# Norm 1 of a hybrid encoder step: five of nine token tiles transposed by DMA instead of by TensorE

## The chip, the cores and the metric

The kernel runs on one core of one Trainium2 chip. A core has five engines with queues of their own: TensorE (PE in the profile, its weight loads PEld), VectorE (DVE), ScalarE (ACT), GpSimd (POOL) and SyncE (SP), which here only issues DMAs. Each works through its own queue in order and waits for the others by semaphores. The DMAs that SP issues run on 16 DMA engines. The metric is the device time of one execution in microseconds (us), the median of several runs.

## The reference

One step of a hybrid streaming encoder layer for 1024 prompt tokens and 64 sample tokens, 1024 features, in float32. Cut to what bears on the change:

```python
def rms_norm(x, g):
    xf = x.astype(F32)
    y = xf * lax.rsqrt(jnp.mean(xf * xf, axis=-1, keepdims=True) + EPS)
    return y.astype(x.dtype) * g

def token_mixers(u, past, p, l):
    proj = u @ p['w_in'][l]                      # 7436 columns
    fox, dif, sb, gdn, gates = jnp.split(proj, SPLITS, axis=-1)
    ...                                          # three attentions and a gated delta rule over them
    merged = sum(gate[:, :, i] * (o @ wb[i]) for i, o in enumerate(branches))
    return merged @ p['w_out'][l], new_state

def trunk(x, caches, p):
        mix, st = token_mixers(rms_norm(x, p['norm1_g'][l]), past, p, l)
        x = x + mix
        x = x + swiglu(rms_norm(x, p['norm2_g'][l]), p['w_ffn_gate'][l], p['w_ffn_up'][l], p['w_ffn_down'][l])
    y = rms_norm(x, p['final_norm_g'])
```

## The kernel before

The tokens form nine tiles: eight of 128 prompt tokens (t = 0 to 7) and one of 64 sample tokens (t = 8). Every float32 operand of a large product is split into two float16 halves, a high part and the remainder, and a product is three matmuls (high by high, high by low, low by high). The products want the normalised input u with features on the partitions, so the kernel keeps it transposed in one buffer, `u1` (line 222), with its halves `uh` and `ul`, 8 blocks of 128 features by 1088 tokens.

Norm 1 is `rms_to` (line 188), called once a tile from the loop at line 237. ACT squares the row and sums it, POOL makes the reciprocal root, DVE multiplies (`u32`, natural layout, tokens on partitions). TensorE then transposes eight 128x128 blocks of `u32` in float32 into two PSUM banks (`ptu`, line 200). From each bank ACT copies the high half into `uh`, and DVE takes the remainder into `ul`. 

Right behind it stands the first user of u, the loop over tiles that makes 268 columns (`gemm_b`, lines 158 to 168; three matmuls for each of eight blocks, 24 a tile, into one of two PSUM buffers `pd`). Its results leave PSUM by two small DVE copies (`abf`, lines 275 and 276) and one ACT copy (`zt`); ACT takes a tanh of that (`zh`), DVE multiplies it twice, and SP writes it to DRAM (`zd`, line 286). `zt` and `zh` share four buffers, so a write that is late holds back a later ACT copy, and that a PSUM buffer. Then follows `gdn_project`, which reads all of u for 768 columns (matmuls of lines 183 to 185).

Beside this run: the loads of x and of weights by SP (lines 230 and 149), the split of weights into halves (`wh` by ACT, `wl` by DVE), and small constants: `gnb`, `lq`, `gsub`, loaded by SP and touched by DVE. The weights land in three buffers `w32`, so a load waits until DVE has split what its buffer held.

The program is written as one stream. A scheduler with a time model of its own then fixes the order in which each engine meets its instructions; that order is part of the built program, and nothing is reordered at run time between the instructions of DVE, ACT, POOL or SP. In the attention phases that follow, projections fill TensorE beside the attention, and DMA transposes like those of the change are in use already (`pt<-st`, `qt<-qd`, `gt<-stg`, and `X<-nsh`, `X<-nsl` in norm 2).

Of the kernel before, what the change touches and what calls it, by code (L numbers as in the profile page):

```python
# [9 lines left out]
F16 = mybir.dt.float16  # L10
# [3 lines left out]
ALU = mybir.AluOpType  # L14
# [3 lines left out]
P = 128  # L18
D = 1024
# [29 lines left out]
def rows(t):  # L49
    return P if t < 8 else SMP  # L50
# [3 lines left out]
def tile_hybrid_encoder(ctx, tc, i, o):  # L54

    nc = tc.nc
    act, vec, gps, pe, sync = nc.scalar, nc.vector, nc.gpsimd, nc.tensor, nc.sync


    def acopy(out, in_, scale=1.0):  # L60
        return act.activation(out, in_, AF.Copy, scale=scale)  # L61

    def stt(out, in0, s, in1, op0, op1):
        return vec.scalar_tensor_tensor(out=out, in0=in0, scalar=s, in1=in1, op0=op0, op1=op1)  # L64

    def tt(out, in0, in1, op, eng=None):
        return (eng or vec).tensor_tensor(out=out, in0=in0, in1=in1, op=op)

    def ts(out, in0, s1, s2, op0, op1=None, eng=None):
        if op1 is None:  # L70
            return (eng or vec).tensor_scalar(out=out, in0=in0, scalar1=s1, scalar2=None, op0=op0)  # L71
        return (eng or vec).tensor_scalar(out=out, in0=in0, scalar1=s1, scalar2=s2, op0=op0, op1=op1)
# [16 lines left out]
    def psc(name="psc"):  # L89
        return pp.tile([P, 512], F32, tag="s", name=name, bufs=3)  # L90
# [50 lines left out]
    def load_unit_(parts, n, kk, wh, wl, w32t=None):  # L141
        wh, wl = (a.rearrange("p (k c) -> p k c", k=8) for a in (wh, wl))
        for k0 in range(0, kk, 4):
            kn = min(4, kk - k0)
            w32 = w32t() if w32t else wp.tile([P, 4, BW], F32, tag="w32", name="w32", bufs=3)
            c = 0
            for src, r0, c0, w in parts:
                with tc.issue_after(ahead[0]) if ahead else ExitStack():
                    sync.dma_start(
                        w32[:, :kn, c:c + w],  # L150
                        src[r0 + k0 * P:r0 + (k0 + kn) * P, c0:c0 + w].rearrange("(k p) c -> p k c", p=P),
                    )
                c += w
            acopy(wh[:, k0:k0 + kn, :n], w32[:, :kn, :n], WS)
            stt(wl[:, k0:k0 + kn, :n], w32[:, :kn, :n], WS, wh[:, k0:k0 + kn, :n], ALU.mult, ALU.subtract)
        return wh, wl
# [28 lines left out]
            mm = pe.matmul(ps[:, :n], lhsT=b, rhs=xh[:, k, off:off + n], start=False, stop=(k == K - 1))  # L185
        return mm

    def rms_to(pool, xt, n, g_bc, outh, outl, tok):

        u32 = pool.tile([P, D], F32, tag="nu", name="u32", bufs=2)  # L190
        ss = pool.tile([P, 1], F32, tag="nss", name="ss", bufs=3)
        act.activation(u32[:n], xt[:n], AF.Square, accum_out=ss[:n])
        rs = pool.tile([P, 1], F32, tag="nrs", name="rs", bufs=3)
        ts(rs[:n], ss[:n], 1.0 / D, EPS, ALU.mult, ALU.add, eng=gps)
        tt(rs[:n], rs[:n], mh[:n], ALU.pow, eng=gps)
        stt(u32[:n], xt[:n], rs[:n], g_bc[:n], ALU.mult, ALU.mult)
        for q in range(2):
            ps = psc("ptu")
            for k in range(4):
                pe.transpose(ps[:, k * P:k * P + n], u32[:n, (4 * q + k) * P:(4 * q + k + 1) * P], ident[:n, :n])  # L200
            pv = ps.rearrange("p (k t) -> p k t", k=4)[:, :, :n]
            hi, lo = (a[:, 4 * q:4 * q + 4, tok:tok + n] for a in (outh, outl))
            acopy(hi, pv)
            tt(lo, pv, hi, ALU.subtract)
# [4 lines left out]
    def xrows(t):  # L209
        return xp[t * P:(t + 1) * P] if t < 8 else xs  # L210
# [12 lines left out]
    uh, ul = u1[:, 0], u1[:, 1]  # L223
    with tc.tile_pool(name="n1", bufs=1, reuse_waits="tile") as n1:
        g1 = n1.tile([P, D], F32, name="g1")
        xts = []
        with tc.high_priority():
            for t in range(NT):
                xt = n1.tile([P, D], F32, tag="xt", name="xt", bufs=6)
                early = sync.dma_start(xt[:rows(t)], xrows(t))  # L230
                xts.append(xt)
                if t == 0:
                    sync.dma_start(g1, i["norm1_g"][0].partition_broadcast(P))
                    wua = load_unit_([(w_in, 0, OFF_ABZ, 264), (w_in, 0, OFF_FOX + 768, 4)], 268, 8,
                                     *(wa.tile([P, 8 * 268], F16, name="wa" + q) for q in "hl"),
                                     lambda: wa.tile([P, 4, 268], F32, tag="wa32", name="wa32", bufs=2))
        for t in range(NT):
            rms_to(n1, xts[t], rows(t), g1, uh, ul, t * P)


    zd = tc.dram_tile([T, BW], F32, name="zd")
# [27 lines left out]
    for t in range(NT):  # L269
        n = rows(t)  # L270
# [45 lines left out]
    for t0, cols in (((0, 1, 2, 3), 0), ((4, 5, 6, 7), 512), ((9, 10, 8), 1024)):  # L316
        ps = psc("pct")
        c = 0
        for t in t0:
            n = SMP if t == 8 else P  # L320
# [792 lines left out]
    for bi, b in enumerate(order):  # L1113
# [18 lines left out]
        for d, (off, n) in [(d, PIECES[p]) for p in (0, 2, 1) for d in range(KD)] if last else \  # L1132
                [(d, p) for d in range(KD) for p in PIECES]:
            th = (brp if bi == 0 else gt_pool).tile([P, 364], F32, tag=("th0" if bi == 0 else "th"), name="thg",
                                                    bufs=(4 if bi == 0 else 12))
# [120 lines left out]
    with tc.tile_pool(name="ps2", bufs=1, space=PSUM) as pf:  # L1256
# [189 lines left out]
        for t in (8, 0, 1, 2, 3, 4, 5, 6, 7):  # L1446
            n = rows(t)
            ss = fp.tile([P, 2], F32, tag="fss", name="fss", bufs=4)
            xh = [x2[t][:n, c * HK:(c + 1) * HK] for c in range(2)]
            dst = o["y_prompt"][0, t * P:(t + 1) * P] if t < 8 else o["y_sample"][0]  # L1450
# [51 lines left out]
```

## Time and profile before

| what | value |
|---|---|
| time, median of 3 runs | 1857.35 us (1855.86 to 1864.47) |
| the profiled execution's own time | 1860.61 us |
| its span | 1858.8 us |
| TensorE busy | 1736.6 us, 93% |
| VectorE busy | 1251.2 us, 67% |
| ScalarE busy | 862.3 us, 46% |
| mean granted TensorE clock | 0.981 of full |

The span is from the first to the last instruction on the core; the execution's own time is 1.8 us longer. Busy shares are means over stages with different limits, so a change in one stage is read from that stage. In a timeline a row gives the start, the duration, the engine, the line, the operation with the tile it writes and the tiles it reads, and, in brackets, how long the engine stood idle before and what ended that. Names are the program's, with numbers left out: `u` stands for u32 and u1 both, which the shapes tell apart.

### The profile page before, as it was taken

The page shows a single profiled execution, that of the slowest core. Times are in us where ns is not written, and L with a number is a line of the kernel's source. Part 1 is how long each engine was busy: PE and PEld are TensorE (multiplying, and loading weights), DVE is VectorE, ACT ScalarE, POOL GpSimd, SP SyncE. Part 2 cuts the span into 40 slices and gives each one's busy share as a digit, 9 for nine tenths or more (in the row PEclk, how much of TensorE's full clock was granted, in tenths as well). Part 3 has the DMA queues.
Part 4 walks back from the last instruction along what each step waited for, and adds up shares of the span by engine and source line. Part 5 has one row for each costly group of instructions (what it writes and reads, how often), then busy time and mean ns, then how long its engine had stood idle before and what let it go on. Part 6 is the DMA issues. An engine that isn't in the chain of part 4 may idle for free.

```text
span 1858.8 us, 36758 instructions
## 1 busy us (share of the span) xinstructions
PE 1736.6 (93%) x14364; PEld 1229.3 (66%) x14364; DVE 1251.2 (67%) x2634; ACT 862.3 (46%) x1819; POOL 291.9 (16%) x443
## 2 busy tenths in 40 slices
PE   7979987788988889999998989999999999999998
PEld 5658875565655556666665578777758668577573
DVE  7547984997877667877746887757637456465465
ACT  6325564977865545655654633523304223133132
POOL 2102240001212212232222731000000000000002
PEclk9989999999999999999999999999999999999999
DMA  7247798889899976655857845512211113012112
GB/s 225 49 71 182 221 252 186 191 188 215 181 203 198 192 153 138 148 141 134 209 178 235 228 141 104 109 52 69 69 35 58 46 46 92 26 44 69 35 46 102
DMA packets 415941, 244.55 MB, mean 132 GB/s; under 512 B 270066, under 2 KB 393422, under 8 KB 415700
## 3 DMA queue, kind: packets, MB, share of 16 engines
q1 hardware_dynamic: 403304, 206.22, 46.2%
q0 software_dynamic: 12464, 35.99, 6.7%
q8 instruction: 112, 1.84, 0.4%
q14 instruction: 61, 0.50, 0.1%
HBM read 123.39 MB, written 60.81 MB: 99 GB/s over the span
## 4 chain that ended last, share of the span: by engine, by line
PE 63%; DMA 13%; DVE 11%; issue 4%; ACT 4%; SPq 2%; POOL 1%; DVEq 0%; POOLq 0%; ACTq 0%
PE po L1424 12%; DMA pt<-st 5%; PE pgs L184 4%; PE pgs L183 4%; PE pgs L185 4%; PE pb L1308 3%; PE pb L1307 3%; PE pb L1309 3%; PE pc L1308 2%; PE pc L1309 2%; PE pa L1309 2%; PE pc L1307 2%; PE pa L1307 2%; PE pa L1308 2%; DMA gt<-stg 2%
## 5 line engine op out<-in xcount | busy, mean ns | idle before, releaser
L183 PE MATMUL pgs<-u,wh 128*128 128x364 f16 (+1 forms) x768 | 245.3, 319 | 0.5 <-ACT ths L61 0.5
L185 PE MATMUL pgs<-u,wl 128*128 128x364 f16 (+1 forms) x768 | 245.2, 319 | 0.0
L184 PE MATMUL pgs<-u,wh 128*128 128x364 f16 (+1 forms) x768 | 245.0, 319 | 0.0
L1424 PE MATMUL po<-wh,hT 128*128 128x512 f16 (+1 forms) x792 | 238.2, 380 | 0.6 <-DVE x2a L64 0.5
L1424 PEld LDWEIGHTS <-hT 128*128 128x128 f16 (+1 forms) x1188 | 109.1, 99 | 120.1 <-issue 7.6
L64 DVE SCALAR_TENSOR_TENSOR x2a<-po,x2a 128x512 f32<-128x512 f32 x108 | 74.4, 689 | 141.1 <-PE po L1424 140.9
L61 ACT ACTIVATE wh<-w32f 128x1024 f16<-128x1024 f32 (+1 forms) x90 | 80.3, 926 | 160.6 <-PE po L1424 111.7
L1307 PE MATMUL pb<-X,wh 128*128 128x288 f16 (+1 forms) x528 | 147.1, 279 | 2.4 <-DMA X<-nsh 2.0
L64 DVE SCALAR_TENSOR_TENSOR wl<-w32f,wh 128x1024 f16<-128x1024 f32 (+1 forms) x90 | 94.6, 1065 | 79.8 <-ACT wh L61 79.8
L1308 PE MATMUL pb<-X,wh 128*128 128x288 f16 (+1 forms) x528 | 147.2, 279 | 0.5 <-DMA X<-nsl 0.5
L1309 PE MATMUL pb<-X,wl 128*128 128x256 f16 (+1 forms) x528 | 146.4, 279 | 0.0
L1424 PE MATMUL po<-wl,hT 128*128 128x512 f16 (+1 forms) x396 | 142.1, 379 | 0.0
L165 PE MATMUL pd<-wh,u 128*128 128x256 f16 (+1 forms) x456 | 128.3, 281 | 14.4 <-DVE ks L64 6.6
L1307 PEld LDWEIGHTS <-wh 128*128 128x128 f16 x1232 | 120.4, 98 | 31.0 <-issue 2.2
L1308 PEld LDWEIGHTS <-wh 128*128 128x128 f16 x1232 | 120.4, 98 | 30.1 <-issue 2.4
L1309 PEld LDWEIGHTS <-wl 128*128 128x128 f16 x1232 | 120.4, 98 | 27.5 <-issue 1.0
L184 PEld LDWEIGHTS <-wh 128*128 128x128 f16 x912 | 89.8, 98 | 60.3 <-issue 11.4
L166 PE MATMUL pd<-wl,u 128*128 128x256 f16 (+1 forms) x456 | 128.0, 281 | 0.0
L167 PE MATMUL pd<-wh,u 128*128 128x256 f16 (+1 forms) x456 | 128.0, 281 | 0.0
L183 PEld LDWEIGHTS <-wh 128*128 128x128 f16 x912 | 89.8, 98 | 50.6 <-issue 1.3
L185 PEld LDWEIGHTS <-wl 128*128 128x128 f16 x912 | 89.8, 98 | 49.8 <-issue 1.2
L71 POOL TENSOR_SCALAR fss<-fss 128x1 f32<-128x1 f32 (+1 forms) x9 | 2.0, 220 | 660.2 <-ACT fsq L1453 660.2
(396 smaller groups left out, 4625.1 us busy)
## 6 DMA issues: line engine op xcount, KB each, us to landing
w<-in_w_in_dram SPq DMA_DIRECT2D x56, 512.0 KB, 4.7
w32f<-in_w_ffn_gate_dram SPq DMA_DIRECT2D x20, 512.0 KB, 5.0
w32f<-in_w_ffn_up_dram SPq DMA_DIRECT2D x20, 512.0 KB, 3.9
w32f<-in_w_ffn_down_dram SPq DMA_DIRECT2D x20, 512.0 KB, 4.8
xt<-in_x_prompt_dram SPq DMA_DIRECT2D x8, 512.0 KB, 6.9
wb<-in_w_branch_dram SPq DMA_DIRECT2D x8, 512.0 KB, 4.6
w<-in_w_out_dram SPq DMA_DIRECT2D x8, 512.0 KB, 3.8
x2a<-in_x_prompt_dram SPq DMA_DIRECT2D x8, 512.0 KB, 6.1
```

Of the source, the lines that this page charges most:

```text
L61: return act.activation(out, in_, AF.Copy, scale=scale)
L64: return vec.scalar_tensor_tensor(out=out, in0=in0, scalar=s, in1=in1, op0=op0, op1=op1)
L165: pe.matmul(ps[:n, :N], lhsT=a, rhs=wh[:, k, :N], start=(k == 0), stop=False)
L166: pe.matmul(ps[:n, :N], lhsT=a, rhs=wl[:, k, :N], start=False, stop=False)
L167: pe.matmul(ps[:n, :N], lhsT=b, rhs=wh[:, k, :N], start=False, stop=(k == K - 1))
L183: pe.matmul(ps[:, :n], lhsT=a, rhs=xh[:, k, off:off + n], start=(k == 0), stop=False)
L184: pe.matmul(ps[:, :n], lhsT=a, rhs=xl[:, k, off:off + n], start=False, stop=False)
L185: mm = pe.matmul(ps[:, :n], lhsT=b, rhs=xh[:, k, off:off + n], start=False, stop=(k == K - 1))
L1307: pe.matmul(ps[:, :n], lhsT=wh[:, k], rhs=xh_, start=(start and k == 0), stop=False, skip_group_check=not start)
L1308: pe.matmul(ps[:, :n], lhsT=wh[:, k], rhs=xl_, start=False, stop=False, skip_group_check=not start)
L1309: mm = pe.matmul(ps[:, :n], lhsT=wl[:, k], rhs=xh_, start=False, stop=(k == 3), skip_group_check=not start)
L1424: pe.matmul(ps[h * n:h * n + n], lhsT=hts[k + h][:, a, tk:tk + n], rhs=w[:, k + h], start=(k == 0 and a == 0 and w is wh), stop=(k + nh >= ...
```

## The change

From tile 4 on, the split comes first and the transpose after it: ACT copies the whole `u32` tile to float16 in natural layout, DVE takes the remainder, and two DMA transposes, issued by SP, put the two halves into `uh` and `ul`. The staging tiles `ust` rotate over six buffers. Tiles 0 to 3 keep the old way.

```diff
-    def rms_to(pool, xt, n, g_bc, outh, outl, tok):
+    def rms_to(pool, xt, n, g_bc, outh, outl, tok, by_dma):
...
         stt(u32[:n], xt[:n], rs[:n], g_bc[:n], ALU.mult, ALU.mult)
+        if by_dma:
+            st = [pool.tile([P, D], F16, tag="nst", name="ust", bufs=6) for _ in range(2)]
+            acopy(st[0][:n], u32[:n])
+            tt(st[1][:n], u32[:n], st[0][:n], ALU.subtract)
+            for dst, src in zip((outh, outl), st):
+                sync.dma_start_transpose(out=dst[:, :, tok:tok + n], in_=src[:n])
+            return
         for q in range(2):
             ps = psc("ptu")
...
         for t in range(NT):
-            rms_to(n1, xts[t], rows(t), g1, uh, ul, t * P)
+            rms_to(n1, xts[t], rows(t), g1, uh, ul, t * P, t >= 4)
```

The scheduler places the new instructions among the old. On SP, behind the load of the constant `gsub`, there stood before the loads of weights (`w32`) and the writes of the first gate tiles (`zd`):

```order
L595 DMA gsub_726<-in_diff_subln_g_dram 128x64
L149 DMA w32_921<-in_w_in_dram 128x4x256
L149 DMA w32_1085<-in_w_in_dram 128x4x256
L286 DMA zd_331<-zt_387 128x256
L286 DMA zd_331<-zt_421 128x256
L149 DMA w32_1089<-in_w_in_dram 128x4x256
L149 DMA w32_1314<-in_w_in_dram 128x4x256
```

In the changed program SP has there, from the second pair of weight loads on (`ust_230` and `ust_231` are the high and low halves of tile 4, `243` and `244` of tile 5, `256` and `257` of tile 6, `269` and `270` of tile 7):

```order
L149 DMA w32_1045<-in_w_in_dram 128x4x256
L149 DMA w32_1049<-in_w_in_dram 128x4x256
L293 DMA zd_291<-zt_347 128x256
L293 DMA zd_291<-zt_381 128x256
L202 DMA_TRANSPOSE u1_103<-ust_244 128x8x128
L202 DMA_TRANSPOSE u1_103<-ust_256 128x8x128
L149 DMA w32_1274<-in_w_in_dram 128x4x256
L293 DMA zd_291<-zt_415 128x256
L202 DMA_TRANSPOSE u1_103<-ust_269 128x8x128
L202 DMA_TRANSPOSE u1_103<-ust_257 128x8x128
L202 DMA_TRANSPOSE u1_103<-ust_270 128x8x128
```

Ten transposes now stand among the loads and the gate writes; the high half of tile 7 is issued ahead of the low half of tile 6. Three more, of tile 4 and of tile 5's high half, stand right before the first of these rows, and the two of tile 8 behind the last.

On DVE, from the constant `lq` on, before (the numbers of `ptu` are the PSUM banks of tiles 5, 6 and 7, `u32_265` and `u32_286` the multiplications of tiles 6 and 7):

```order
L67 TENSOR_TENSOR lq_715<-lq_715 128x64
L67 TENSOR_TENSOR u1_103<-ptu_230,u1_103 128x4x128
L71 TENSOR_SCALAR gsub_726<-gsub_726 128x64
L67 TENSOR_TENSOR u1_103<-ptu_237,u1_103 128x4x128
L275 TENSOR_SCALAR abf_350<-pd_462 128x8
L276 TENSOR_SCALAR abf_350<-pd_462 128x4
L67 TENSOR_TENSOR zt_387<-zt_387,gnb_357 128x256
L67 TENSOR_TENSOR zt_421<-zt_421,gnb_357 128x256
L589 TENSOR_REDUCE lam_721<-lq_715 128x2
L64 SCALAR_TENSOR_TENSOR u32_265<-xt_133,rs_268,g1_107 128x1024
```

The same place on DVE in the changed program, where `wl` is the split of a weight tile and `u32_249` the multiplication of tile 6:

```order
L67 TENSOR_TENSOR lq_675<-lq_675 128x64
L71 TENSOR_SCALAR gsub_686<-gsub_686 128x64
L64 SCALAR_TENSOR_TENSOR wl_708<-w32_713,wh_707 128x1024
L282 TENSOR_SCALAR abf_310<-pd_422 128x8
L283 TENSOR_SCALAR abf_310<-pd_422 128x4
L64 SCALAR_TENSOR_TENSOR wl_876<-w32_877,wh_875 128x1024
L67 TENSOR_TENSOR zt_347<-zt_347,gnb_317 128x256
L67 TENSOR_TENSOR zt_381<-zt_381,gnb_317 128x256
L596 TENSOR_REDUCE lam_681<-lq_675 128x2
L67 TENSOR_TENSOR ust_244<-u32_236,ust_243 128x1024
L64 SCALAR_TENSOR_TENSOR zt_415<-zh_417,zt_415 128x256
L64 SCALAR_TENSOR_TENSOR u32_249<-xt_133,rs_252,g1_107 128x1024
```

Two weight splits now stand between `lq` and the low half of tile 5, and that half stands ahead of the multiplication of tile 6. On PE the 36 float32 transposes of the five tiles are gone, and the matmuls keep their order but for four of tile 7 that move up to where tile 6 begins. Behind this stage SP's order is the same for more than fifty DMAs and PE's for more than 2,000 rows; after that all engines meet the projections and the attention in a somewhat different order.

## Rows read from the trace of the kernel before

**Rows 1.** The page: span, and busy time of each engine.
```profile
span 1858.8 us, 36758 instructions
PE 1736.6 (93%) x14364; PEld 1229.3 (66%) x14364; DVE 1251.2 (67%) x2634; ACT 862.3 (46%) x1819; POOL 291.9 (16%) x443
```

**Rows 2.** Busy time by stage: start:end length, engines, PEclk, DMA share, GB/s.
```profile
core 0: us, PE busy (x) PEld busy (x) DVE busy (x) ACT busy (x) POOL busy (x), PEclk, DMA share, GB/s
0.00:50.20 50.20, 38.44 (x288) 30.83 (x288) 37.06 (x78) 30.92 (x61) 9.73 (x26) 0.97 0.68 216
50.20:113.00 62.80, 62.80 (x419) 40.74 (x419) 29.82 (x62) 18.22 (x39) 9.65 (x15) 1.00 0.45 63
...
290.00:490.00 200.00, 162.58 (x1562) 119.28 (x1561) 160.05 (x282) 150.62 (x290) 18.18 (x29) 0.94 0.87 194
490.00:640.00 150.00, 134.98 (x1495) 87.84 (x1493) 106.31 (x334) 92.25 (x220) 33.12 (x53) 0.97 0.96 196
```

**Rows 3.** The same view: two stretches of norm 1, one of norm 2.
```profile
30.00:40.00 10.00, 8.79 (x63) 7.30 (x64) 9.67 (x21) 5.98 (x13) 2.08 (x4) 0.83 0.72 222
40.00:50.00 10.00, 9.67 (x86) 8.09 (x83) 8.10 (x23) 4.22 (x11) 0.00 (x0) 1.00 0.24 79
1184.00:1186.00 2.00, 0.18 (x2) 0.16 (x2) 2.00 (x4) 0.00 (x0) 0.00 (x0) 1.00 0.96 181
```

**Rows 4.** Timeline of PE in norm 1.
```profile
24.64 1.04 PE L200 MATMUL ptu<-ident,u 128*128 128x128 f32 x8
25.51 0.28 PE L167 MATMUL pd<-wah,u 128*128 128x268 f16 x1
...
28.03 0.60 PE L200 MATMUL ptu<-ident,u 128*128 128x128 f32 x4
...
31.21 1.08 PE L200 MATMUL ptu<-ident,u 128*128 128x128 f32 x4 [2.35 <-DVE u L67]
32.08 0.43 PE L167 MATMUL pd<-wah,u 128*128 128x268 f16 x1
...
34.74 0.28 PE L167 MATMUL pd<-wah,u 128*128 128x268 f16 x1
...
50.21 0.33 PE L183 MATMUL pd<-u,wh 128*128 128x364 f16 x1
```

**Rows 5.** Timeline of DVE in norm 1.
```profile
26.46 2.35 DVE L64 SCALAR_TENSOR_TENSOR wl<-w,wh 128x1024 f16<-128x1024 f32 x2
28.73 0.19 DVE L71 TENSOR_SCALAR gnb<-gnb 128x64 f32<-128x64 f32 x1
30.33 0.23 DVE L67 TENSOR_TENSOR lq<-lq 128x64 f32<-128x64 f32 x1 [1.42 <-issue]
...
40.99 1.26 DVE L64 SCALAR_TENSOR_TENSOR u<-xt,rs,g 64x1024 f32<-64x1024 f32 x1
```

**Rows 6.** Groups by line and shape, 0 to 52 us: count, busy, mean ns.
```profile
L67 DVE TENSOR_TENSOR u<-ptu,u 128x512 f16<-128x512 f32 x16 | 10.5, 678 | 0.0
L61 ACT ACTIVATE u<-ptu 128x512 f16<-128x512 f32 x16 | 9.1, 599 | 5.8 <-PE ptu L200 5.8
```

**Rows 7.** The tile nsh of norm 2: duration ns min/median/max, then landing.
```profile
L1207 SPq DMA_TRANSPOSE X<-nsh x15: 1176/1232/1476, 1105.0 to 1182.0; - x15
L61 ACT ACTIVATE nsh<-ua x5: 1040/1057/1057, 1103.9 to 1166.2; 128x1024 f16<-128x1024 f32 x4, 32x1024 f16<-32x1024 f32 x1
L67 DVE TENSOR_TENSOR nsl<-ua,nsh x5: 1206/1219/1226, 1106.0 to 1169.0; 128x1024 f16<-128x1024 f32 x4, 32x1024 f16<-32x1024 f32 x1
...
DMA to landing us min/median/max: 2.3/3.1/5.6
```

**Rows 8.** The tile pt of the attention phases: landing of its 108 transposes.
```profile
DMA to landing us min/median/max: 2.3/4.1/13.2
```

**Rows 9.** Timeline of SP in norm 1.
```profile
26.46 0.43 SPq L595 DMA_DIRECT2D gsub<-in_diff_subln_g_dram  x1
27.70 1.51 SPq L149 DMA_DIRECT2D w<-in_w_in_dram  x2
```

**Rows 10.** Timeline of ACT in norm 1.
```profile
24.24 2.01 ACT L61 ACTIVATE wh<-w 128x1024 f16<-128x1024 f32 x2
26.13 0.39 ACT L61 ACTIVATE zt<-pd 128x256 f32<-128x256 f32 x1
```

## The prediction

> **What bounds the kernel now.** I read the page first, then the busy time by stage, then the timelines of norm 1. The page says that TensorE is busy for 1736.6 of 1858.8 us [rows 1], a mean over stages that differ. By stage, norm 1 with the gate columns (0 to 50.2 us) has TensorE busy for 38.4 of 50.2 us; in the next 62.8 us, `gdn_project`, it is busy all the time [rows 2]. So whatever norm 1 gains or loses up to the start of `gdn_project` at 50.21 us [rows 4] is handed to a stage that has no slack on TensorE, and later stages hang on that one in turn. I carry it to the end one for one.
>
> Inside norm 1, DVE is the busiest engine from 30 to 40 us, 9.67 of 10 us; TensorE has 8.79, at a mean granted clock of 0.83 [rows 3]. The timeline shows why: TensorE waits 2.35 us for DVE before the second half of tile 5's transposes at 31.21 us, and what follows runs at the lower clock level, 1.2 GHz: the matmuls take 0.43 us each instead of 0.28 until 34.74 us, when the 2.4 GHz level is back [rows 4]. DVE itself had stood until 30.33 us before `lq`, in its own queue [rows 5]. Its order and its load, not the transposes, set the pace of tiles 5 to 8.
>
> **What goes.** A tile's eight fp32 transposes hold TensorE from 24.64 to 25.51 us, 0.87 us [rows 4]; for four tiles and a half that is 3.9 us. Two PSUM reads of 0.599 us on ACT become one copy of 1.057 us; two of 0.678 us on DVE become one subtraction of 1.219 us [rows 6, 7]. Per tile ACT and DVE each save 0.14 us: nothing that I count, since each instruction's start follows the one before a little closer than these durations say, in both forms.
>
> **What comes.** Ten transposes, 1.23 us of SP each [rows 7], so 12.3 us in SP's queue; SP waited most of this stretch and can carry them, but each stands in line. A transpose of 128 by 1024 float16 (256 KB) lands 3.1 us after its issue, between 2.3 and 5.6 [rows 7]. Where TensorE had its result in PSUM some 0.9 us after DVE's multiplication and ACT and DVE worked behind it, now ACT and DVE work first and SP and the flight come last, with TensorE behind them.
>
> **The chain that sets the end, step by step.** Up to the wait for `lq` both programs are alike but for ACT's copy and DVE's subtraction of tile 4. That copy follows the first weight copy (24.24 plus 1.0 [rows 10]) and ends near 26.2; the subtraction follows one weight split and ends near 28.6; SP issues it at 28.9, behind `gsub` [rows 9], one transpose and one load; it lands at 32.0. Tile 4's matmuls start at 32.08 us before [rows 4], so tile 4 is even. The load of 27.70 us is issued at about 28.2: nobody needs it before 32.
>
> From `lq` at 30.33 on, DVE has the same work as before, in another order, and one weight split more, the second of the pair at 26.46 us that stood ahead of `lq` (1.17 us each [rows 5]). Before, it had finished tile 7's second half when tile 8's multiplication started, at 40.99 us [rows 5]. The low half of tile 7 is now at the same point of the work, so it ends at 40.99 + 1.17 = 42.2 us less the small ones that it has moved past: 42.0. The low half of tile 6 stands one gate product (about 0.3) and one subtraction (1.2) earlier, at 40.5 us.
>
> SP issues the high half of tile 7 first, at about 40.4 us (ACT's copy follows tile 7's multiplication at once). Then come low 6 at 41.7 and low 7 at 42.9, each 1.23 us behind the one before. They land 3.1 us later: 44.8 and 46.0 us.
>
> TensorE, with tile 5 done at about 41 us (its low half leaves DVE at 34.9, lands at 38.2, and 22 matmuls take 2.5 us: 25.51 to 28.03 in [rows 4]), has four early matmuls and then waits until 44.8. Waits of this length lowered the clock at 31.21 for 3.5 us; I take the same here, at half speed from the early matmuls on, which costs 1.1 us. Tile 6: 44.8 + 2.5 + 1.1 = 48.4. Tile 7: 22 matmuls, 50.9. Tile 8: 24 matmuls, 2.75 us, 53.7. Its own low half leaves DVE near 46.4, is issued at 46.9 and lands at 50.0, so it is hidden by 0.9 us. The stage ends at 53.7 instead of 50.2 us: 3.5 us later. The 3.9 us that TensorE saved are spent waiting.
>
> **Bounds.** With the shortest landing (2.3) and no fall of the clock, tile 6 starts at 44.0 and the end is 51.8: 1.6 us late. With the longest of norm 2 (5.6), low 6 lands at 47.3, the low half of tile 8 at 52.5, and the end is 55.3 to 57.9: up to 7.7 late. One landing like the longest of the attention phases, 13.2 us [rows 8], would put it at 62 or so. Two things pull landing up. The ten transposes move 2.36 MB, and with the DMA engines 0.96 busy on transposes alone they moved 181 GB/s [rows 3]: 13.0 us of all engines. From 28.9 to 50 us about 10 us of them are free (0.28 of the time up to 40, 0.76 after [rows 3]), most of it behind 40 us, where low 6 to low 8 fly. So I stay near the median of [rows 7], add half a microsecond for a landing of 3.6, and take 4 us.
>
> The Trainium skill, in "DMA: Bandwidth & Descriptors" (Latency and other measured facts), gives a transposing DMA 261 GB/s. [Rows 3] has 181 GB/s for this form, at a busy share of 0.96, so the trace does not bear the page's figure out. By the page, as an estimate, a tile half would take 0.4 us less of the DMA engines and the loss would be near 3.5 us instead of 4.
>
> **The sum.** The profiled execution took 1860.61 us, its span 1858.8 plus 1.8; with 4 us more it would take 1864.6. It lies 3.3 us over the median of the runs, 1857.35. On the median I forecast 1861.4, say 1861 us, slower by 0.2%. That is less than what a measurement of this kernel can tell from no change, about 0.5% or 9.3 us.
>
> **Rivals.**
> 1. *Transposes queue among loads and writes.* Place: SP's queue and the DMA engines, 30 to 50 us. Each pair lands 5 to 7 us after its issue, and `zd` writes queued behind the transposes hold the gate buffers, so ACT's `zt` and the two `pd` banks come free late. For it: DMA share 0.72 between 30 and 40 us [rows 3] and a longest landing of 13.2 us [rows 8]. Against: the share falls to 0.24 behind 40 us [rows 3]. Price 6.4 to 12 us: 1864 to 1869, centre 1867. Chance 0.20.
> 2. *TensorE was the pace after all: faster.* Place: tiles 5 to 8. If DVE, freed from waiting for PSUM, brings the low half of tile 7 before about 37 us, the 3.9 us of transposes, the wait of 2.35 and the slow stretch go: 3.5 us at half speed, 1.7. Price up to 8 us: 1849 to 1856, centre 1852. It decides at `lq`: DVE must reach it without the stand of 1.42 us and keep fewer than 6 us of work between `lq` and the low half of tile 7. Against: 9.67 of 10 us busy, and DVE's work has not shrunk. Chance 0.12.
> 3. *The order behind decides.* The scheduler's order differs in the attention phases, where the DMA engines are busy for 0.87 to 0.96 of the time [rows 2] and one landing can cost 13 us [rows 8]. One or two such landings more or fewer on the chain are 10 to 20 us, of either sign: 1843 to 1877. For it: hundreds of places changed. Against: the same work and the same dependencies. Chance 0.13, three fifths of it slower.
>
> That the change does not do what it says is excluded by the order: the float32 transposes of five tiles are gone and ten DMA transposes stand in SP's queue.
>
> **How the numbers follow.** The forecast has 0.55, with a range of its own from 1858 to 1865. Slower by over 0.5% (above 1866.6) is half of rival 1 and 0.08 of rival 3: 0.18. Faster by over 0.5% (below 1848.1) is less than half of rival 2, 0.05, and 0.05 of rival 3: 0.10. Within 0.5%: 0.72. The range of 1851 to 1871 holds the forecast, most of rival 1 and half of rival 2, and leaves out the ends of rival 3.
>
> **What would show it.** In the changed profile: `gdn_project`'s first matmul (the line of 183, seven lines further down) at 53 to 54 us; TensorE waiting for a DMA into `u` before tile 5 and before tile 6, 1 to 4 us each, with a granted clock below 1 between 30 and 50 us; DVE's subtraction of tile 7 ending near 42 us; the transposes of `ust` landing 3 to 4 us after issue. Wrong would be a first matmul before 50 us (rival 2), after 57 us (rival 1), or one at 53 us beside an end that is off by more than 8 us (rival 3).

## The result, and the profile after

| | before | changed |
|---|---|---|
| median of 10 runs, us | 1856.34 | 1874.84 |
| lowest and highest | 1852.12, 1864.47 | 1863.93, 1881.91 |
| profiled execution, its span, us | 1860.61, 1858.8 | 1874.38, 1872.6 |

The ratio is 1.0088 (95% interval 1.0067 to 1.0109): slower by 0.9%, outside the forecast range of 1851 to 1871 us.

The page after, the rows that answer to [rows 1]: TensorE has 40 matmuls fewer (eight transposes for each of five tiles, 40 and not the 36 that the section on the change counts) and is still busy 4.6 us longer.
```profile
span 1872.6 us, 36691 instructions
PE 1741.2 (93%) x14324; PEld 1230.5 (66%) x14324; DVE 1252.4 (67%) x2629; ACT 861.8 (46%) x1814; POOL 292.7 (16%) x443
```

Busy time by stage after, over the same stretches and with the same columns as [rows 2] and, for the two stretches of norm 1, [rows 3]:
```profile
0.00:50.20 50.20, 30.10 (x200) 22.30 (x201) 35.34 (x65) 29.76 (x52) 10.83 (x26) 0.90 0.92 253
50.20:113.00 62.80, 61.49 (x421) 40.83 (x420) 32.23 (x71) 19.24 (x42) 9.65 (x15) 1.00 0.37 59
...
290.00:490.00 200.00, 165.31 (x1571) 123.17 (x1570) 160.56 (x284) 150.09 (x291) 18.19 (x29) 0.94 0.87 199
490.00:640.00 150.00, 134.73 (x1493) 88.11 (x1492) 102.70 (x324) 90.84 (x214) 32.28 (x51) 0.95 0.92 191
...
30.00:40.00 10.00, 4.85 (x26) 3.13 (x26) 9.30 (x18) 4.05 (x8) 3.45 (x4) 0.66 1.07 238
40.00:50.00 10.00, 6.82 (x45) 4.92 (x46) 6.39 (x12) 4.83 (x9) 0.79 (x2) 0.83 1.06 228
```
Up to 50.2 us TensorE is busy for 8.3 us less, and the DMA share is over 1 in both stretches where before it was 0.72 and 0.24. Nothing like that is seen in the later stages: there the sums look alike, and the loss is to be found by where each stage begins.

TensorE's timeline in norm 1 after (start, length, line, tile; in brackets the wait ahead of it), answering to [rows 4]:
```profile
30.95 0.29 PE L165 MATMUL pd<-wah,u 128*128 128x268 f16 x1 [3.76 <-DMA u<-ust]
...
35.24 0.40 PE L167 MATMUL pd<-wah,u 128*128 128x268 f16 x1 [3.89 <-DMA u<-ust]
...
38.50 0.28 PE L167 MATMUL pd<-wah,u 128*128 128x268 f16 x1
...
42.27 0.40 PE L167 MATMUL pd<-wah,u 128*128 128x268 f16 x1 [2.58 <-DMA u<-ust]
...
54.85 0.30 PE L167 MATMUL pd<-wah,u 128*64 128x268 f16 x1 [0.95 <-DMA u<-ust]
...
57.49 0.33 PE L183 MATMUL pd<-u,wh 128*128 128x364 f16 x1
```
`gdn_project` begins at 57.49 instead of 50.21 us. The waits stand ahead of the high and the low half of tile 4 (30.95 and 35.24 us), of the low half of tile 5 (42.27) and of tile 8 (54.85). Twice such a wait, of 3.89 and 2.58 us, is followed by matmuls of 0.40 us: TensorE's 1.2 GHz level.

SP's queue after, in the stretch that [rows 9] begins:
```profile
29.19 4.82 SPq L202 DMA_TRANSPOSE u<-ust  x2
34.10 1.08 SPq L149 DMA_DIRECT2D w<-in_w_in_dram  x2
35.28 1.60 SPq L293 DMA_DIRECT2D zd<-zt  x2
36.97 4.04 SPq L202 DMA_TRANSPOSE u<-ust  x2
41.10 0.53 SPq L149 DMA_DIRECT2D w<-in_w_in_dram  x1
41.73 0.45 SPq L293 DMA_DIRECT2D zd<-zt  x1
42.27 4.97 SPq L202 DMA_TRANSPOSE u<-ust  x3
...
51.21 2.14 SPq L202 DMA_TRANSPOSE u<-ust  x1
```
DVE after, where [rows 5] has tile 8's multiplication at 40.99 us:
```profile
42.23 1.23 DVE L67 TENSOR_TENSOR ust<-u,ust 128x1024 f16<-128x1024 f32 x1 [0.52 <-ACT ust L61]
...
46.43 0.17 DVE L282 TENSOR_SCALAR abf<-pd 128x8 f32<-128x8 f32 x1 [2.63 <-PE pd L167]
...
46.91 1.27 DVE L64 SCALAR_TENSOR_TENSOR u<-xt,rs,g 64x1024 f32<-64x1024 f32 x1
...
49.31 1.22 DVE L67 TENSOR_TENSOR ust<-u,ust 64x1024 f16<-64x1024 f32 x1
```
The tile `ust`, answering to [rows 7]: durations on SP in ns (min/median/max), then the landing.
```profile
L202 SPq DMA_TRANSPOSE u<-ust x10: 1192/1539/3484, 27.1 to 51.2; - x10
...
DMA to landing us min/median/max: 3.1/4.2/6.0
```
So the end of norm 1 is made like this. Tile 4's low half is issued at 29.19 us and lands only at 35.2, and the transpose behind it (tile 5's high half) holds SP for 3.48 us, up to 34.0. Tile 5's subtraction starts at 33.23 us and its low half is issued at 36.97, behind two weight loads and two `zd` writes as well; it lands at 42.2. TensorE does tile 5 slowly, DVE's `abf` waits for that until 46.43, tile 8's multiplication stands behind `abf`, and tile 8's low half goes out at 51.21 and lands at 54.8.

But in the traces the 7.3 us do not travel on as they are. In what follows, `dT` is a tile of the gated delta rule, `pgs` the gate projection, which TensorE does between its other work, `pv` and `po` the products of the attention weights with the values in the attention called fox (428 to 668 us before) and in the one called diff (668 to 979 us), and `pt` those weights, transposed by DMA. This table has the start of the first instruction of each kind (the last row: the end), from the four traces named; the two on the right belong to the first two experiments.

| us | before | changed | new norm 1, old order | old norm 1, new order |
|---|---|---|---|---|
| `gdn_project`'s first matmul | 50.2 | 57.5 | 57.4 | 53.4 |
| DVE's first product into `dT` | 113.7 | 114.0 | 113.5 | 116.0 |
| first `pgs` (gate projection) | 427.8 | 435.5 | 432.1 | 434.4 |
| first `po` (diff attention) | 668.3 | 669.6 | 668.6 | 671.4 |
| end of the last `pgs` | 978.2 | 992.6 | 979.4 | 994.1 |
| first `pout` | 1081.2 | 1094.8 | 1082.1 | 1096.3 |
| end of the span | 1858.8 | 1872.6 | 1861.4 | 1875.3 |

DVE's first product into `dT` waits for the two loads of `dT`, which read back from DRAM what POOL has sent there (`gcd`). Before:
```profile
113.67 2.56 DVE L67 TENSOR_TENSOR dT<-dT,gc 128x2304 f32<-128x2304 f32 x1 [12.96 <-DMA dT<-gcd]
```
and after:
```profile
113.96 2.56 DVE L67 TENSOR_TENSOR dT<-dT,gc 128x2304 f32<-128x2304 f32 x1 [5.96 <-DMA dT<-gcd]
```
The loads are issued 7.5 us later in the changed kernel, at 104.19 instead of 96.71 us, since what they read is worked out from the 268 columns, which end later; but they land sooner after their issue. The view of the tile `dT`, before:
```profile
DMA to landing us min/median/max: 16.1/16.1/16.1
```
and after:
```profile
DMA to landing us min/median/max: 9.0/9.0/9.0
```
So the delay is gone at `dT` because this landing took 7.1 us less, not because the chain had time to spare. Why it took less stays open. It goes with the kernel: 8.9 to 9.4 us in all ten kernels here with ten or more of the new transposes, 13.6 to 16.2 us (the later of the two loads) in all nine with eight or none.

Behind `dT` TensorE had idle time before (columns as in [rows 2]):
```profile
114.00:135.00 21.00, 12.15 (x75) 7.94 (x74) 12.58 (x13) 6.80 (x11) 1.52 (x2) 0.76 0.03 5
```
and has little after:
```profile
114.00:135.00 21.00, 18.43 (x118) 11.95 (x116) 12.86 (x13) 6.79 (x11) 1.52 (x2) 0.92 0.40 37
```
TensorE carries 6.3 us more of work into this stretch, and finds 8.85 us of idle time there. At 114 us the changed kernel is 0.3 us late. From there to the first `pgs` it loses 7.4 us, from the first `pgs` to the first `po` it wins 6.4, and from there to the last `pgs` it loses 13.1, in stages where the change has edited nothing. In the program, 791 matmuls of `pgs` (of 2304) stand ahead of the first `po` before and 759 after: 32 of them have moved behind it, some 5 us of TensorE's time: a row of `pgs` lasts 0.32 us, but the next starts 0.155 us after it. What differs is the order: of the 14153 TensorE instructions traced behind norm 1, 5183 stand in another place.

### The profile page after: what moved, and what is told of

Read it like the earlier page. It is cut to its first block, busy times and chain, and to the rows that moved or that the text cites. A ratio compares the mean times of both kernels' runs of the same rounds, so it can differ in the third digit from the quotient of the medians.

```text
span 1872.6 us, 36691 instructions
## 1 busy us (share of the span) xinstructions
PE 1741.2 (93%) x14324; PEld 1230.5 (66%) x14324; DVE 1252.4 (67%) x2629; ACT 861.8 (46%) x1814; POOL 292.7 (16%) x443
## 4 chain that ended last, share of the span: by engine, by line
PE 64%; DMA 14%; DVE 11%; issue 4%; ACT 3%; SPq 2%; POOL 1%; DVEq 0%; POOLq 0%; ACTq 0%
PE po L1431 12%; DMA pt<-st 5%; PE pgs L184 4%; PE pgs L185 4%; PE pgs L183 4%; PE pb L1314 3%; PE pb L1315 3%; PE pb L1316 3%; PE pc L1315 2%; PE pa L1316 2%; PE pa L1314 2%; PE pa L1315 2%; PE pc L1314 2%; PE pc L1316 2%; DMA gt<-stg 2%
```

## The experiments

All pinned kernels use one device: every instruction traced behind norm 1 (19,522 of them, the same ones in both kernels) gets a chain of issue-order edges on its engine, in the order that the other kernel has. "Old order" is that of before, "new order" that of the changed kernel.
```
+        for a, b in zip(row, row[1:]):
+            tc.add_manual_dep(b, a.name, mybir.DependencyInfo(mybir.DependencyClass.NoSync, mybir.DependencyReason.DATA),
+                              reason="pin_order")
```
Here `row` is one engine's instructions behind norm 1 in the wanted order, and the edge fixes the order of issue alone, without a wait. The edges by themselves cost nothing that the runs show: `before_filled` of group 6, pinned to the order of before but for 17 matmuls, measured 1.0002 (0.9983 to 1.0022). Each kernel was timed in five rounds beside before; ratios are to before, with 95% intervals. Traces are of one execution each.

**1. Norm 1 and the order apart.** `new_norm_old_order` is the changed kernel with the old order:

> The changed norm 1 (tiles 4 to 8 by DMA), with every instruction traced behind norm 1 pinned, on each engine, to the order it has in the kernel before. Theory 1 (the order behind norm 1 costs the time; the later end of norm 1 is taken up by the wait at 113 us): first matmul of the gdn projection again at 56 to 58 us, the first dT multiply at 113 to 115, and a time of 1854 to 1861 us, a ratio to before of 0.999 to 1.002. Rival (the late end of norm 1 is carried to the end): 1863 us or more, ratio 1.004 or more.

Measured: 1.0036 (1.0016 to 1.0056), 1864.93 us. First gdn matmul at 57.4, `dT` at 113.5, as theory 1 has it; but the ratio lies between the two theories and the median on the rival's side. The one profiled execution is only 2.5 us longer than that of before, which lies 4 us over its own median. The interval reaches from 3 to 10 us: norm 1 has at most a part in the loss, and how much of its 7.2 us of delay this kernel carries to the end it does not tell. `old_norm_new_order` is before with the new order:

> Norm 1 of the kernel before (all nine tiles by TensorE), with every instruction traced behind norm 1 pinned, on each engine, to the order it has in the changed kernel. Theory 1: first matmul of the gdn projection at 50 to 51 us as before, and still a time of 1868 to 1878 us, ratio 1.007 to 1.011. Rival (norm 1 is the cause): 1853 to 1860 us, ratio 0.998 to 1.002.

Measured: 1.0110 (1.0085 to 1.0135), 1879.36 us. **The reordering alone makes a loss as large as the whole one**: nothing of norm 1's computation has changed in this kernel. (Its first gdn matmul is at 53.4 us, not 50: the new order also touches what runs beside norm 1.) The two parts do not add up: 0.36 and 1.10% apart, 0.88% together.

**2. More and fewer tiles.**
```
-            rms_to(n1, xts[t], rows(t), g1, uh, ul, t * P, t >= 4)
+            rms_to(n1, xts[t], rows(t), g1, uh, ul, t * P, t >= 5)   # five_to_eight; all_nine_old_order: t >= 0 and the old order
```


> Only tiles 5 to 8 by DMA, nothing pinned. On paper its order behind norm 1 differs from that of before in some 770 of 14153 TensorE places, that of the changed kernel in some 5180. Theory 1: first gdn matmul later than 52 us, and yet a time near the kernel before, 1855 to 1864 us, ratio 0.999 to 1.004. Rival (norm 1 is the cause, in proportion to the tiles moved): 1868 to 1874, ratio 1.006 to 1.010.

Measured: 1.0071 (1.0047 to 1.0095), the rival's number. Its order is neither of the two, and its `dT` comes at 120.9 us, since the later of the two loads landed only 15.1 us after its issue; so it tells the theories apart less well than I had thought.

> All nine tiles by DMA, the order behind norm 1 pinned to that of before: a larger dose of the delay alone. Theory 1 with slack of about 8 us at the dT wait: first gdn matmul at 62 to 72 us, of which what goes beyond 58 is carried to the end, so 1858 to 1870 us. Rival (no slack, the whole delay is carried): the first gdn matmul's delay against 50.2 us is found again in full at the end, 1868 to 1880 us.

Measured: 1.0059 (1.0037 to 1.0082), first gdn matmul at 69.4 us. That is 19.2 us later than before, and the time is 7 to 15 us longer: a delay of norm 1 is not carried to the end one for one. Beside `new_norm_old_order` it is 12.0 us later there, 12.5 at `dT` (both loads take 9 us), and 5.5 at the end of the span: in these two executions half of what is still late at `dT` is taken up further on.

**3. Which stretch of the order.** All four have the changed norm 1; the order changes over at the first `pgs` or the first `po`. My theory F rested on these waits of TensorE, before (428 to 668 us; in total, times, longest):
```profile
PE pv L468 <- DMA pt<-st: 8.3, 4, 3.7
```
and after (435.5 to 669.2 us):
```profile
PE pv L475 <- DMA pt<-st: 15.9, 10, 3.2
```


> Changed norm 1; behind it the changed kernel's order up to the first matmul that writes po (668 us in the trace of before), from there the order of the kernel before. Theory F (the new order does less gate projection between the fox scores and their pv, 759 instead of 791 matmuls of pgs ahead of po, so TensorE waits there for pt and does them later): nearly all of the new order's loss is already made at the cut, ratio to before 1.007 to 1.011, waits of pv for pt 14 us or more between the first pgs and the first po. Rival D (the order of the diff phase itself is worse): ratio 1.002 to 1.006.

Measured: 1.0053 (1.0033 to 1.0072): rival D.

> Changed norm 1; behind it the order of the kernel before up to the first po, from there the changed kernel's order. Theory F: like the changed norm 1 with the old order throughout, ratio 1.002 to 1.006, waits of pv for pt below 10 us. Rival D: 1.008 to 1.012, and more than 318 us from the first po to the last pgs (310 in before, 323 in the changed kernel).

Measured: 1.0106 (1.0064 to 1.0149): rival D, though the stretch from the first `po` took 316.7 us, a little less than it asked.

> Changed norm 1; the changed kernel's order up to the first matmul of the gate projection (pgs, 428 us in the trace of before), from there the order of before. Theory F: the fox stretch keeps its old filler, pv waits for pt below 10 us there, ratio 1.002 to 1.006. Rival P (the loss is made in the projections of 157 to 428 us, by waits for gt and a lower clock, and stays): 1.007 to 1.011.

Measured: 1.0100 (1.0072 to 1.0128): rival P.

> Changed norm 1; the order of before up to the first matmul of the gate projection, from there the changed kernel's order. Theory F: loses as the changed kernel does, ratio 1.006 to 1.010, pv waits for pt 14 us or more. Rival P: ratio 1.001 to 1.005.

Measured: 1.0060 (1.0035 to 1.0085), at the lower end of what theory F asked; but `pv` waited only 8.2 us for `pt`, not 14. Theory F falls: the fox stretch of the new order is not where the time goes. Taking it up made the kernel faster in both comparisons (1.0100 to 1.0053; 1.0106 to 1.0060), the stretches on its two sides made it slower.

**4. The same with norm 1 of before**, so that nothing but the order of one stretch differs from before.

> Norm 1 of before; the changed kernel's order only up to the first matmul of the gate projection (428 us), the order of before behind it. With the new order throughout the ratio was 1.0110, only between 428 and 668 us 1.0013, only behind 668 us 1.0063. Theory A (the stretches add up): 1.0025 to 1.0045 here. Rival M (a seam between the two orders costs as such): 1.006 or more, as the same order had with the changed norm 1 (1.0100).

Measured: 1.0051 (1.0028 to 1.0074), some 9.5 us, between the two theories. In this kernel the new order delays norm 1 itself: the first gdn matmul is at 56.0 us and `dT` at 117.5, so 3.8 us of the loss are there at `dT`.

> Norm 1 of before; the order of before up to the first gate projection matmul (428 us) and from the first po (668 us) on, the changed kernel's order only between them. Theory A (each stretch's order has a price of its own: in the six kernels with the new norm 1 the new order cost about +0.6% before 428 us, -0.5% from 428 to 668, +0.7% behind): ratio to before 0.993 to 0.998, some 8 us faster than before. Rival M (any mixture of the two orders costs, the order of before is best as a whole): 1.002 to 1.008.

Measured: 1.0013 (0.9995 to 1.0031). Theory A's gain of half a per cent is not there; the version that it promised is no faster than before. Nor does changing over between the orders, here twice, cost anything clear of noise.

> Norm 1 of before and its order up to the first po (668 us); only what stands behind has the changed kernel's order. Theory A: ratio 1.005 to 1.009, TensorE's idle time from the first po to the last pgs 9 to 11 us, where it is 4.2 in before, in waits of po for pt. Rival N (the loss comes from norm 1's late end, the order behind 668 us is free): 0.998 to 1.002.

Measured: 1.0063 (1.0048 to 1.0078), as theory A had it. The three stretches give 0.51, 0.13 and 0.63%, in sum 1.27, against 1.10 (0.85 to 1.35) for all: with norm 1 of before they add up within the intervals. Half of the loss is made behind 668 us. The wait of TensorE that grows there is this one. Before (668 to 979 us):
```profile
PE po L602 <- DMA pt<-st: 6.9, 3, 5.4
```
and in `old_norm_new_diff` (660 to 976 us):
```profile
PE po L602 <- DMA pt<-st: 13.0, 6, 4.2
```
From its first `po` to its last `pgs` TensorE is busy for this long (length, busy, clock, DMA share, GB/s), before:
```profile
668.30:978.20 309.90, 305.68 (x2645) 0.99 0.63 157
```
and in `old_norm_new_diff`:
```profile
660.80:980.20 319.40, 307.74 (x2644) 0.98 0.61 152
```
Of 9.5 us more, 7.4 are idle time (11.7 against 4.2 us). As I read it, an uncovered wait is dearest here because TensorE is full otherwise: nothing behind it takes the time in, as the idle time behind 114 us does for norm 1.

In the changed kernel itself the wait is no longer than before (669 to 993 us):
```profile
PE po L609 <- DMA pt<-st: 7.1, 4, 2.3
```
and TensorE's stretch there is
```profile
669.60:992.60 323.00, 312.80 (x2680) 0.98 0.60 153
```
Of its 13.1 us more than before, 7.1 are busy time (some 5 of them the 32 matmuls of `pgs` that moved there) and 6.0 idle time. So that waits for `pt` make the changed kernel's loss behind 668 us is not shown; that its order does is.

**5. Why norm 1 ends at 57 us and not at 53.7.** `four_to_seven` gives tile 8 back to TensorE (`4 <= t < 8`), old order:

> Tiles 4 to 7 by DMA, tile 8 by TensorE again, the order of before behind norm 1. Theory T (the end of norm 1 at 57.4 us, not the 53.7 forecast, is tile 8's: its multiply stands on VectorE behind the abf of an earlier tile that waits for transposed data, so its low half is issued only at 51.2): first gdn matmul at 52 to 55 us. Rival L (every transpose is late by its landing, 4.2 us where 3.1 was taken): 56 to 58 us still. Time against before: 1.001 to 1.005 by either, since the wait for dT takes up the rest.

Measured: first gdn matmul at 57.7 us (rival L); time 1.0111 (1.0095 to 1.0128), which neither expected. Its `dT` lands only at 119.6 us, 6.1 us later than in `new_norm_old_order`, with the same order and nearly the same end of norm 1. The loads are issued 1.6 us later, and the landing takes 13.6 us instead of 9.1:
```profile
DMA to landing us min/median/max: 13.6/13.6/13.6
```
So without the shorter landing the delay of norm 1 is still there at `dT`. At the end the kernel is some 14 us slower than `new_norm_old_order`, more than these 6.1 us: the landing is then at most a part of its loss, and the rest is open. Why the landing differs I cannot say. `zd_on_pool` takes the `zd` writes out of SP's queue, old order:
```
-        sync.dma_start(zd[t * P:t * P + n], zt[:n])
+        gps.dma_start(zd[t * P:t * P + n], zt[:n])
```


> Changed norm 1 (tiles 4 to 8 by DMA) with the order of before behind it, and the nine writes of zd issued by POOL instead of SP. Theory Q (transposes stand on SP behind zd writes that themselves wait for VectorE and ACT): SP issues the low halves up to 2.5 us earlier, first gdn matmul at 53 to 55.5 us. Rival L (landing time decides): 56.5 to 58 us. Time against before 1.000 to 1.006 by either.

Measured: 58.6 us, 1.0041 (1.0022 to 1.0060). Neither tile 8 nor the `zd` writes alone set the end. That left the clock and the landings. `kept_busy` adds work that is not used, to hold the clock:
```
+    wps = pso("warm")
+    for _ in range(sum(WARM.values())):
+        warm.append(pe.matmul(wps[:, :268], lhsT=uh[:, 0, 0:P], rhs=wua[0][:, 0, :268], start=True, stop=True).ins)
```
`WARM` is 40, 12 and 40: so many stand in TensorE's order ahead of the 268 columns ("abz" below) of tiles 4, 5 and 6.

> Changed norm 1 with the order of before behind it, and 92 extra matmuls (128x268, result not used) put on TensorE ahead of the abz projections of tiles 4, 5 and 6 (40, 12, 40), where it otherwise waits for transposes. Theory C (in the same kernel without them the granted clock reads 0.50 and 0.72 behind those waits and a tile's 24 matmuls take 5.1 and 5.0 us instead of 2.7): with the extra matmuls the clock stays near 1.0 and the first gdn matmul comes at 53.5 to 55.5 us, though TensorE has 10 us more to do. Rival L (the landings alone set it): 57 us or later.

TensorE in `new_norm_old_order` (length, busy, granted clock, DMA share, GB/s):
```profile
30.00:40.00 10.00, 5.32 (x24) 0.51 1.15 227
40.00:50.00 10.00, 5.85 (x39) 0.84 1.07 245
```
and in `kept_busy`:
```profile
30.00:40.00 10.00, 7.18 (x64) 1.00 1.12 231
40.00:50.00 10.00, 8.55 (x76) 1.00 1.08 239
```
The clock was held. The start of tile 6's low products in `new_norm_old_order`:
```profile
47.75 0.41 PE L167 MATMUL pd<-wah,u 128*128 128x268 f16 x1 [1.60 <-DMA u<-ust]
```
and in `kept_busy`, with the first gdn matmul:
```profile
48.79 0.29 PE L168 MATMUL pd<-wah,u 128*128 128x268 f16 x1 [1.45 <-DMA u<-ust]
...
57.03 0.33 PE L184 MATMUL pd<-u,wh 128*128 128x364 f16 x1
```
At full clock the rest takes 8.2 us instead of 9.6, but low 6 landed 1.0 us later. So rival L has the stage: with low 6 landing at 47.7 to 48.8 us instead of the 44.8 forecast, three tiles of work remain and the end is at 57. The time, however, was 1.0004 (0.9986 to 1.0023), where `new_norm_old_order` had 1.0036: with `gdn_project` 6.8 us late, at most 4.3 us are left at the end. I asked the same under the changed kernel's own order:

> The changed kernel with its own order, and the 92 extra matmuls of kept_busy ahead of the abz projections of tiles 4 to 6. With the order of before the ratio went from 1.0036 without them to 1.0004 with them. Theory K (the fall of the clock in norm 1 is the part of the loss that norm 1 itself makes): 1.004 to 1.007. Rival O (under the new order norm 1 costs nothing anyway, since the old norm 1 in that order measured 1.0110): 1.008 to 1.011.

Measured: 1.0080 (1.0049 to 1.0110), beside 1.0088 without: rival O. The clock of norm 1 has no part in the loss of the changed kernel that these runs can tell. Why the extra matmuls seemed to help under the old order stays open; the two intervals overlap.

**6. Covering the waits.** `diff_filled` is `old_norm_new_diff` with `pgs` matmuls drawn forward on TensorE, `before_filled` is before with 17 of them. Both edits lie in the order table alone: matmuls of `pgs` are taken from their later places and put ahead of a group of `po`. In `diff_filled` the table has 25 of them moved, not the 36 that I expected: 13 ahead of the first group, none ahead of the second, 8 and 4 ahead of the third and the fourth. They also fill less than expected: 17 matmuls of `pgs` at 0.155 us from start to start are 2.6 us, not the 5.4 of their durations, and 25 are 3.9 us.

> Norm 1 of before, its order up to the first po, the changed kernel's order behind it, as in old_norm_new_diff; only on TensorE 36 matmuls of pgs are drawn forward ahead of four groups of po (13, 11, 8, 4, as long as each waited: 4.2, 3.5, 2.6, 1.3 us). Theory W (the order behind 668 us costs what po waits for pt uncovered): ratio to before 0.999 to 1.003, idle time from the first po to the last pgs down to 3 to 6 us. Rival E (the waits only move elsewhere): 1.005 to 1.008 as without.

The first three waits for `pt` that were to be covered, in `old_norm_new_diff`:
```profile
660.78 0.29 PE L602 MATMUL po<-vt,pt 128*128 128x128 f16 x1 [4.22 <-DMA pt<-st]
...
668.75 0.29 PE L602 MATMUL po<-vt,pt 128*128 128x128 f16 x1 [3.54 <-DMA pt<-st]
...
853.35 0.23 PE L602 MATMUL po<-vt,pt 128*128 128x128 f16 x1 [2.60 <-DMA pt<-st]
```
and in `diff_filled`:
```profile
660.77 0.23 PE L602 MATMUL po<-vt,pt 128*128 128x128 f16 x1 [2.81 <-DMA pt<-st]
...
668.44 0.29 PE L602 MATMUL po<-vt,pt 128*128 128x128 f16 x1 [3.32 <-DMA pt<-st]
...
849.73 0.23 PE L602 MATMUL po<-vt,pt 128*128 128x128 f16 x1 [1.17 <-DMA pt<-st]
```
The second, ahead of which nothing was put, stays as it is. Measured: 1.0032 (1.0009 to 1.0054), between the two theories; the waits for `pt` are 8.9 us in sum instead of 13.0, the idle time in the stretch 9.5 us, not 3 to 6 (in the fastest of twelve executions). The ratio is half of that without the filler, but the two intervals touch, so that covered waits give back time is likely and not shown.

> The kernel before in its own order, but 17 matmuls of pgs (0.319 us each) drawn forward ahead of the first po, which waits 5.4 us for pt in the trace of before. Theory W: up to 5.4 us gained, 1850 to 1855 us, ratio 0.997 to 0.9995. Rival E (pt lands when it lands and what follows is late in another place): 0.9995 to 1.002.

Measured: 1.0002 (0.9983 to 1.0022). The wait, 5.43 us in before, became two:
```profile
666.94 0.23 PE L602 MATMUL po<-vt,pt 128*128 128x128 f16 x1 [2.88 <-DMA pt<-st]
...
675.70 0.29 PE L602 MATMUL po<-vt,pt 128*128 128x128 f16 x1 [2.92 <-DMA pt<-st]
```
The first is shorter by 2.55 us, as much as the 17 matmuls fill; the second was not there before. Rival E: 5.8 us in sum. The filler that is used up here is missing at the next group. No version beat the kernel before.

## Why the prediction was wrong

**The failed step** is the sum: it has norm 1 as its only term and none for the order behind it, which was left to rival 3 with a chance of 0.13. With the 7.3 us that norm 1 really took in place of the 4, the sum would have come to 1864.7 us, still inside the range. The order, with norm 1 as it was, costs 1.10% (0.85 to 1.35), some 20 us; the changed norm 1 without the new order costs 0.36% (0.16 to 0.56). "For it: hundreds of places changed" was too little: it is 5183 of 14153 on TensorE and 1068 of 2546 on DVE. "Against: the same work and the same dependencies" was the error: the same work in another order took 1.1% longer, as I read it because the order decides which waits it covers. Rival 3's price of 10 to 20 us came out, its reason is not shown: it counted on landings of 13 us on the chain, and the longest wait for `pt` in `pv` or `po` was 3.2 us in the changed kernel and 4.2 us, in `po`, in `old_norm_new_diff`.

**A second step failed**, "whatever norm 1 gains or loses ... I carry it to the end one for one": `all_nine_old_order` was 19.2 us late and lost 7 to 15 us, `kept_busy` was 6.8 us late and lost at most 4.3. TensorE was full up to 113 us, as said, but the stage behind was not, and the prediction does not look there. In the traces two things took the delay in: the loads of `dT` landed 7.1 us sooner after their issue, and TensorE did the 6.3 us of work that it had carried over in the 8.85 us of idle time between 114 and 135 us. The first seems to decide: in `four_to_seven`, where the landing stayed long, `dT` came 6.1 us later and the loss was 1.11%.

**The stage was mis-sized**, 7.3 us for 3.5, by two terms, SP's queue and the landing. Tile 4 was not even: its low half was issued at 29.19 (forecast 28.9) and landed at 35.2, where 32.0 was forecast. SP: low 5 left DVE at 34.4 (forecast 34.9) but was issued at 36.97 and landed at 42.2, where 38.2 was forecast; low 6 was issued at 44.24 and landed at 47.9, for 41.7 and 44.8. The landing: 4.2 us in the median with the DMA share at 1.07, for 3.1 where it was taken from. The step that tile 8's low half would be "hidden by 0.9 us" failed in the changed kernel (it landed at 54.8, not 50.0), but `four_to_seven` shows that without it the end is no earlier. The clock was treated about rightly: a fall behind the waits was in the sum, though for one stretch and not for two.

One reading of the kernel before was off by a tile. `ptu_230` and `ptu_237` in the section on the change are banks of tile 4, and when tile 8's multiplication started at 40.99 us, DVE had finished tile 6. Tile 7's two halves are the last of the 16 such rows:
```profile
42.66 1.27 DVE L67 TENSOR_TENSOR u<-ptu,u 128x512 f16<-128x512 f32 x2
```
It did little harm, since three tiles' remainders stand between `lq` and that point in either kernel: tile 7's low half left DVE at 43.46, for 42.0 in the forecast.

**Right** were the waits for the DMA into `u`, though they stood ahead of tiles 4 and 5 (3.76, 3.89 and 2.58 us) and hardly of tile 6 (0.35 us), the landing of 3 to 4 us, nearly (4.2 in the median), the granted clock below 1, and that the change saves TensorE nothing. Rival 1 had the stage ("after 57 us") and a part of its reason, the place behind loads and writes in SP's queue, but not landings of 5 to 7 us for each pair, and not the path to the end. For the changed norm 1 alone the forecast of 4 us, a ratio of 1.0022, lies in the interval measured (1.0016 to 1.0056), by luck: the stage was twice as late, and a part of it was taken up.

The Trainium skill, in "VectorE: DVE Perf Modes" (Rules for kernel authors), tells to transpose 128x128 on TensorE if the result may go to PSUM, and by DMA otherwise. The runs agree as far as norm 1 goes: with four, five and nine tiles transposed by DMA `gdn_project` began at 55.7, 57.5 and 69.4 us instead of 50.2, and no such kernel was faster than before.

**Open**: which feature of the new order loses the 0.5% ahead of 428 us; why the loads of `dT` land after 9 us in some kernels and after 14 to 16 in others; why the fox stretch of the new order measured faster with the new norm 1 (1.0100 to 1.0053) and not with the old one (1.0013); and which engine's order matters, which was not tried, since the engines' orders hang on one another.

## What to carry to other kernels

Where a scheduler places the instructions, an edit in one stage re-deals all that follow: count the places that move, price the reordering as a term of its own (here 1.1% for over a third of TensorE's rows), and pin the old order in an experiment before blaming or praising the edit. Before a delay is carried to the end, look for the next stretch in which the full engine is idle, and for what ends that idle time; if that does not come later too, the delay can end there. Filler drawn forward to cover one wait can be missing at the next: look at the sum of the waits, not at the one.

## What the runs showed of the hardware

- The ten DMA transposes of norm 1 (eight of 256 KB, two of 128 KB) landed 3.1/4.2/6.0 us after their issue (min/median/max) with weight loads beside them at a DMA share of 1.07, against 2.3/3.1/5.6 in norm 2 [rows 7], whose sizes are mixed too; the longest held SP for 3.48 us, where the median in norm 2 is 1.23.
- The same two loads of `dT` (576 KB each) landed 8.9 to 9.4 us after their issue in the ten kernels with ten or more of the new transposes, and 13.6 to 16.2 us (the later of the two) in the nine with eight or none.
- With 92 unused matmuls in TensorE's waits the granted clock read 1.00 from 30 to 50 us, where it read 0.51 and 0.84 without them.
- The delay of all nine transposed tiles, 19.2 us at `gdn_project`'s start, was 8.1 us at the end of the span (one execution each; by the ratio 7 to 15 us).
